# Softmax factors moved into the queries, and no scaling of the row maxima

## The chip, the cores and the metric

The kernel runs on one core of one Trainium2 chip. The metric is device time in microseconds (us), from one launch; three runs of the kernel before took 1216.63 to 1222.46 us, median 1217.19. Engines are named as in the profile: PE (TensorE), PEld (its weight loads), DVE (VectorE), ACT (ScalarE), POOL (GpSimd), SP (SyncE, which issues most DMAs).

## The reference

Two blocks on 256 tokens of 1024 features, all in fp32. The first block has two layers, each a softmax attention and a squared-ReLU MLP; the second has a gated feed-forward layer, a mixer (a state-space product beside a latent attention) and another gated layer. Three attentions appear, and each scales its logits before the softmax:

```python
# layer 0 (16 heads of 64): scale = 1/sqrt(64)
s_own = einsum('bhcd,bhkd->bhck', qc, k_own) * scale - slopes * dist_own       # causal
# layer 1: scale = 1/sqrt(64), c = running sum of log forget gates
sc = einsum('bhqd,bhkd->bhqk', qb, k) * scale + cq[..., None] - c[:, :, None, :]  # causal
# latent attention (8 heads of 64 + 32): scale = 1/sqrt(96)
q = (rmsnorm(cq, q_norm_w) @ w_uq)
s = (einsum(q_nope, k_nope) + einsum(q_rope, k_rope)) * scale                     # causal
p = softmax(s); out = p @ v
```

## The kernel before, in words

Every product with a weight is made in three passes of float32r (hi hi, hi lo, lo hi), by token (lines 212 to 214) or by feature (245 to 247). So each slab of weights, 128x1024 values, is loaded by SP into `raw` (line 147, five buffers), cast by ACT to `wh` and subtracted to `wl`: lines 174 and 175 without a gain, 178 and 179 with one. The subtraction of line 175 is done by DVE, or by POOL for the slabs listed in `on_pool`; the output weights of both attention layers are mostly such. At most five slabs are made ahead of PE.

The program is written out in one order for all engines, and each engine takes its instructions in that order. Big products go on, and side chains (generators) advance by a step at each `tick()`. An attention is such a chain. It works by halves of a PSUM bank of scores: six halves per group of 8 heads (four heads with 128 keys, or two with 256), two groups per layer, and six halves for the latent attention, 30 in all. One half goes through these steps:

- PE makes the scores from `qT` and `kT` (line 607; 1276 in the latent attention).
- DVE adds bias and mask from PSUM to SBUF, `pr` (622, 629 or 1283), takes the negative row maxima `m` (532), and multiplies them by the softmax factor (534). Up to here the logits are 8 (or sqrt(96)) times too large.
- ACT takes the exponentials with that factor as `scale`, and their sums `sm` (537).
- DVE takes the reciprocals (541, or 551 in the latent attention). In the first block POOL then divides (542).
- PE transposes `pr` (547), ACT copies the result to `pT` (549), and PE multiplies by the values (641; 567 in the latent attention).

`queries` (711) moves queries and keys from PSUM to SBUF and multiplies them by the tokens' norms, one [128, 512] tile at a time: 4 tiles of q and 4 of k in each of the two layers. In layer 1 `forget_bias` makes the running sums of the log forget gates times 8 (`lf8`, `ACT.mul(c, p, 8.0)`). In the mixer `latent_chain` makes 1/rms of the latents of queries (`rq`) and of keys (`rk`).

Between the attentions lie MLPs; beside their weights DVE adds up the second block's modulation (485), which POOL sums over the partitions (490). At their end line 846 adds the MLP to the residual `h`.

Of the kernel before, what the change touches and what calls it, by code (L numbers as in the profile page):

```python
# [12 lines left out]
AF = mybir.ActivationFunctionType  # L13
# [3 lines left out]
S = 256  # L17
# [11 lines left out]
def kernel(ctx: ExitStack, tc: tile.TileContext, a: dict, out: bass.AP):  # L29
# [68 lines left out]
    def finish(*some):  # L98
        """Emits what is left of these chains."""
        while any(s in sides for s in some):  # L100
            for s in some:
                if s in sides:
                    advance(s)

    def after_all(*some):
        """Waits for these chains."""
        while any(s in sides for s in some):
            yield 1

# [9 lines left out]
    def slab(w, r0, nk, c0, n, gain=None, m=None, early=0):  # L119
        """Rows r0 .. r0+128*nk and columns c0 .. c0+n of w, in parts of m rows of blocks, the first few split early,  # L120
        into tiles that are free then."""
# [12 lines left out]
    def load_ahead(most=RB):  # L134
        while at["dma"] < min(len(plan), at["prep"] + most):
# [10 lines left out]
            if at["dma"]:  # L146
                nc.sync.dma_start(raw, src)
            else:
                # the first product waits for no more than it needs
                for k in range(src.shape[1]):  # L150
                    nc.sync.dma_start(raw[:, k], src[:, k])
# [32 lines left out]
    def take(i):  # L184
        """Slab i, and more made ready behind it."""
# [19 lines left out]
    def by_t(xT, t):  # L205
        """The stationary operands of token tile t: [(hi, lo)] by k."""
        return [(x[0][:, j, tok(t)], x[1][:, j, tok(t)]) for x in xT for j in range(4)]

    def part(p, xs, ws, first, last):
        """p += x @ w, by token."""  # L210
# [5 lines left out]
    def by_token(idx, xs, ps, first=True, last=True, token_first=False, after=None, before=None):  # L216
        """ps[t] += x[t] @ slab; xs[t]: [(hi, lo)] by k."""
# [15 lines left out]
    def by_feature(idx, xT, ps, before=None):  # L233
        """ps: [128, 2, 256] each; (x @ w)^T, by blocks of 128 columns of w."""
        k = 0
        for i in idx:
            if before is not None:
                before(k)
            for wh, wl in take(i):
                xh, xl = (z[:, k % 4, :] for z in xT[k // 4])  # L240
                for n in range(2 * len(ps)):
                    c = slice(n * TP, (n + 1) * TP)
                    o = ps[n // 2][:, n % 2, :]
                    # the bank's first product clears both halves' flags, so the other half's first overwrites
# [12 lines left out]
    def split(hi, lo, src):  # L257
        """An activation, split into two exact parts."""
# [12 lines left out]
    def transposed(bl, tag):  # L271
        """Up to 4 [128, 128] blocks, transposed and split; returns [(hi, lo)] by block."""
# [13 lines left out]
    def hidden_part(q):  # L286
        """Hidden activations [128, 2, 256], split: [(hi, lo)] by block."""
# [12 lines left out]
    def mean_square(parts, n, eps=EPS):  # L300
        """mean of squares along the free axis, plus eps."""
# [18 lines left out]
    def warm(func):  # L320
        """Has ScalarE load the table of a function ahead of its use."""
# [9 lines left out]
    def log1p_of(e, shape):  # L331
        """log(1 + e) for 0 <= e <= 1, as 2 atanh(e / (2 + e))."""
# [23 lines left out]
    def columns(n, parts, queue):  # L356
        """Rows of 128 values as columns: [128, n]."""
# [15 lines left out]
    def keep_warm(n):  # L373
        """TensorE's clock is at half speed until it has been busy for some microseconds."""
# [25 lines left out]
    def plan_hidden(ups, w_down, cuts, rate, early=0, after=0):  # L400
        """Weights of the cuts of a hidden layer; each cut's last product is one step behind its first ones."""
# [64 lines left out]
    ada = {}  # L466

    def ada_begin(n):
        """The bias in one partition, nothing in the others."""
# [28 lines left out]
    def modulation(j):  # L498
        """A shift, gain or gate of a sublayer, on every partition."""
# [13 lines left out]
    # ticks between the halves of an attention, and within each: before its logits, sums, transposes and products  # L513
# [4 lines left out]
    def attention(halves_, scores, biased, values, put, ready_v=lambda: True, pace=None, give=None):  # L518
        """halves_: (t, n heads, key); scores(i) emits the scores of half i (and says which others it made);
        biased(i, pr, sc) their logits and scale; values(i) the values; put(i, o, rs) takes the products.  # L520
        With give, the probabilities are divided by their sums and given to it by twos of halves, transposed."""
# [3 lines left out]
        def half(s):  # L525
# [4 lines left out]
            scale = biased(s, pr, sc.pop(s))  # L530
            m = tt((TP, nh), "m")
            DVE.tensor_reduce(out=m, in_=pr, axis=AX.X, op=OP.max, negate=True)
            if scale != 1.0:
                DVE.tensor_scalar(m, m, scale, None, op0=OP.mult)
            sm, rs = tt((TP, nh), "sm"), tt((TP, nh), "rs")
            for i in range(nh):
                ACT.activation(out=pr[:, i, :], in_=pr[:, i, :], func=AF.Exp, bias=m[:, i:i + 1], scale=scale,
# [52 lines left out]
    # ================= the first block =================  # L590
    HALVES = [(0, 4, 0, 0), (0, 4, 0, 1), (1, 2, 0, 0), (1, 2, 0, 1), (1, 2, 4, 0), (1, 2, 4, 1)]

    def heads_attention(g, q, k, v, bias, mixT):
        """8 heads of 64 of group g; q, k: by 4 heads, [128, 2, 256]; v: by key tile."""
# [20 lines left out]
        def biased(i, pr, sc):  # L615
            t, nh = HALVES[i][:2]
            if bias is None:
                # 8 * (q k / 8 - slope * distance), causal
                d = dist if t == 1 else dist[:, TP:S]
                for j in range(nh):  # L620
                    slope = 2.0 ** (-8.0 * (8 * g + head(i, j) + 1) / H)
                    DVE.scalar_tensor_tensor(out=pr[:, j, :], in0=d, scalar=-8.0 * slope, in1=sc[:, j, :],
                                             op0=OP.mult, op1=OP.add)
                return 0.125
            # 8 * (q k / 8 + c[query] - c[key]), causal
# [5 lines left out]
            return 0.125  # L631

        def give(i, pT):
            # the values of each head of a pair on a half of the columns: the products come out transposed
# [20 lines left out]
    def attention_layer(layer, ids, xT, vs, chains, next_chain):  # L655
        """xT, vs: made by chains[t][s]; next_chain(t, s): what follows on each part of the residual."""
# [938 lines left out]
```

## Time and profile before

| | |
|---|---|
| runs of the kernel before | 1216.63, 1217.19, 1222.46 us |
| profiled execution: span | 1219.5 us (the page gives no other time of this execution) |
| PE busy | 1174.3 us, 96% |
| DVE busy | 865.2 us, 71% |
| ACT busy | 650.9 us, 53% |
| POOL busy | 304.3 us, 25% |
| mean granted clock of PE | 0.984 of full speed |

The page tells busy time of each engine, the span in 40 slices, the DMA queues, the chain of work that ended last and the costliest groups of instructions. A row of a timeline has the start and the duration in us, then engine, line, operation and tiles; a bracket at its end is the idle time of that engine just before, and what ended it. [...]

### The profile page before, as it was taken

To read this page: it belongs to the slowest core of one execution; us is meant where nothing else is said; L and a number is where in the kernel's file an instruction comes from. 1 tells how busy PE (TensorE), PEld (TensorE's weight loads), DVE (VectorE), ACT (ScalarE), POOL (GpSimd) and SP (SyncE) were. 2 spreads that over 40 slices of the span, in tenths; PEclk is the share of its full clock that TensorE was granted. 3 is DMA by queue.
4 is the path that set the end of the run, shared out by engine and by line. 5 is a ranking of instruction groups with operands and counts; after the bars stand their busy time and mean duration, and the time that the engine had idled before them with its cause. 6 is when DMAs were issued, how large, how long until landed. Compare 5 with 4: busy or idle time off the path is not lost.

```text
span 1219.5 us, 19985 instructions
## 1 busy us (share of the span) xinstructions
PE 1174.3 (96%) x7669; PEld 1059.2 (87%) x7669; DVE 865.2 (71%) x1218; ACT 650.9 (53%) x1115; POOL 304.3 (25%) x260
## 2 busy tenths in 40 slices
PE   8999999999999999999989999998998999999997
PEld 8977989988899789989878999988987787899996
DVE  6665678887677568778777877756776776766445
ACT  6565665445555665455545444545765564444443
POOL 3054202133002511211153112154136405111002
PEclk9999999999999999999989999999998999999999
DMA  8642467886553347878846888853632263777650
GB/s 277 194 127 99 157 226 236 274 275 223 184 172 123 105 130 235 288 264 299 284 143 214 292 268 312 276 176 118 220 89 88 93 226 111 270 232 228 222 189 36
DMA packets 128479, 243.04 MB, mean 199 GB/s; under 512 B 8515, under 2 KB 16612, under 8 KB 128384
## 3 DMA queue, kind: packets, MB, share of 16 engines
q1 hardware_dynamic: 126688, 239.96, 59.7%
q0 software_dynamic: 1376, 1.28, 0.5%
q8 instruction: 60, 0.98, 0.3%
q10 hardware_dynamic: 320, 0.53, 0.1%
q14 instruction: 35, 0.29, 0.1%
HBM read 240.65 MB, written 1.09 MB: 198 GB/s over the span
## 4 chain that ended last, share of the span: by engine, by line
PE 64%; DVE 16%; ACT 6%; DMA 6%; issue 5%; POOL 3%; SPq 0%; POOLq 0%; ACTq 0%; DVEq 0%
PE mm L247 8%; PE mm L246 8%; PE mm L245 8%; PE acc L212 7%; PE acc L213 7%; PE acc L214 7%; DVE wl L179 4%; DMA raw<-in_w_down_dram 3%; PE acc L245 3%; PE acc L247 3%; PE acc L246 3%; DVE wl L175 2%; ACT wh L174 2%; PE mm L213 2%; PE mm L212 2%
## 5 line engine op out<-in xcount | busy, mean ns | idle before, releaser
L174 ACT CAST wh<-raw 128x1024 fp32r<-128x1024 f32 (+1 forms) x231 | 237.7, 1041 | 221.0 <-DMA raw<-in_w_down_dram 67.2
L175 DVE TENSOR_TENSOR wl<-raw,wh 128x1024 fp32r<-128x1024 f32 (+1 forms) x193 | 257.8, 1350 | 137.2 <-ACT wh L174 134.8
L247 PE MATMUL mm<-xh,wl 128*128 128x256 f32 x1088 | 309.3, 284 | 4.4 <-DVE wl L179 4.3
L245 PE MATMUL mm<-xh,wh 128*128 128x256 f32 x1088 | 309.1, 284 | 0.1
L246 PE MATMUL mm<-xl,wh 128*128 128x256 f32 x1088 | 308.4, 283 | 0.0
L179 DVE SCALAR_TENSOR_TENSOR wl<-raw,cols,wh 128x512 fp32r<-128x512 f32 (+1 forms) x270 | 204.0, 806 | 68.0 <-ACT wh L178 64.5
L247 PEld LDWEIGHTS mm<-xh,wl 128*128 128x128 f32 x1088 | 209.3, 192 | 5.9 <-DVE wl L179 5.9
L245 PEld LDWEIGHTS mm<-xh,wh 128*128 128x128 f32 x1088 | 209.3, 192 | 1.3 <-ACT wh L178 0.6
L246 PEld LDWEIGHTS mm<-xl,wh 128*128 128x128 f32 x1088 | 209.3, 192 | 0.7
L178 ACT ACTIVATE wh<-raw,cols 128x512 fp32r<-128x512 f32 (+1 forms) x270 | 175.3, 708 | 64.5 <-PE acc L246 20.1
L212 PE MATMUL acc<-wh,mh 128*128 128x512 f32 x524 | 207.6, 396 | 0.0
L213 PE MATMUL acc<-wl,mh 128*128 128x512 f32 x524 | 205.4, 392 | 0.0
L214 PE MATMUL acc<-wh,ml 128*128 128x512 f32 x524 | 205.1, 391 | 0.0
L490 POOL PARTITION_ALL_REDUCE ada<-ada x18 | 66.4, 3690 | 352.1 <-DVE ada L485 153.4
L175 POOL TENSOR_TENSOR wl<-raw,wh 128x1024 fp32r<-128x1024 f32 (+1 forms) x38 | 91.4, 2407 | 138.9 <-ACT wh L174 132.3
L214 PEld LDWEIGHTS acc<-wh,ml 128*128 128x128 f32 x524 | 99.0, 189 | 21.1
L212 PEld LDWEIGHTS acc<-wh,mh 128*128 128x128 f32 x524 | 98.9, 189 | 20.8 <-issue 1.7
L213 PEld LDWEIGHTS acc<-wl,mh 128*128 128x128 f32 x524 | 99.1, 189 | 19.0 <-DVE wl L175 0.2
L485 DVE SCALAR_TENSOR_TENSOR ada<-raw,c_act,ada 128x512 f32<-128x512 f32 x144 | 107.7, 748 | 2.5
L245 PE MATMUL acc<-xh,wh 128*128 128x256 f32 x352 | 102.0, 290 | 0.0
L246 PE MATMUL acc<-xl,wh 128*128 128x256 f32 x352 | 99.5, 283 | 0.0
L247 PE MATMUL acc<-xh,wl 128*128 128x256 f32 x352 | 99.5, 283 | 0.0
(318 smaller groups left out, 1673.5 us busy)
## 6 DMA issues: line engine op xcount, KB each, us to landing
raw<-in_w_ada_dram SPq DMA_DIRECT2D x72, 512.0 KB, 5.4
raw<-in_w_up_dram SPq DMA_DIRECT2D x64, 512.0 KB, 4.9
raw<-in_w_down_dram SPq DMA_DIRECT2D x64, 512.0 KB, 5.7
raw<-in_ffn_w_gate_dram SPq DMA_DIRECT2D x44, 512.0 KB, 4.7
raw<-in_ffn_w_up_dram SPq DMA_DIRECT2D x44, 512.0 KB, 4.7
raw<-in_ffn_w_down_dram SPq DMA_DIRECT2D x44, 512.0 KB, 5.2
raw<-in_moba_w_qkv_dram SPq DMA_DIRECT2D x23, 512.0 KB, 5.0
raw<-in_w_in_dram SPq DMA_DIRECT2D x20, 512.0 KB, 4.1
```

What stands on the lines that cost most here:

```text
L174: ACT.copy(hi, raw)
L175: (POOL if i in on_pool else DVE).tensor_tensor(lo, raw, f(hi), op=OP.subtract)
L178: ACT.mul(hi[:, k], raw[:, k], gain[k])
L179: DVE.scalar_tensor_tensor(out=lo[:, k], in0=raw[:, k], scalar=gain[k], in1=f(hi[:, k]), op0=OP.mult, op1=OP.subtract)
L212: PE.matmul(p, lhsT=xh, rhs=wh, start=first and n == 0, stop=False)
L213: PE.matmul(p, lhsT=xh, rhs=wl, start=False, stop=False)
L214: PE.matmul(p, lhsT=xl, rhs=wh, start=False, stop=last and n == len(ws) - 1)
L245: PE.matmul(o, lhsT=wh[:, c], rhs=xh, start=k == 0 and n % 2 == 0, stop=False)
L246: PE.matmul(o, lhsT=wh[:, c], rhs=xl, start=False, stop=False)
L247: PE.matmul(o, lhsT=wl[:, c], rhs=xh, start=False, stop=k == 7 and n % 2 == 1)
L485: DVE.scalar_tensor_tensor(out=acc, in0=raw[:, i, :], scalar=c_act[:, k:k + 1], in1=acc, op0=OP.mult, op1=OP.add)
L490: POOL.partition_all_reduce(acc, acc, TP, ReduceOp.add)
```

## The change

The factor 1/8 of the first block's attentions moves into the queries, at the instruction that takes them out of PSUM; keys go through the same instruction with a factor of 1. The bias of layer 0 and the sums of layer 1 lose their factor 8. The factor 1/sqrt(96) moves into the latent queries' norm (96 under the root). The row maxima are then right as they are: line 534 goes, and the exponentials have no `scale`. Comments of the kernel also change; they are left out below.

```diff
             pr = sb("pr", (TP, nh, (t + 1) * TP))
-            scale = biased(s, pr, sc.pop(s))
+            biased(s, pr, sc.pop(s))
             m = tt((TP, nh), "m")
             DVE.tensor_reduce(out=m, in_=pr, axis=AX.X, op=OP.max, negate=True)
-            if scale != 1.0:
-                DVE.tensor_scalar(m, m, scale, None, op0=OP.mult)
             sm, rs = tt((TP, nh), "sm"), tt((TP, nh), "rs")
             for i in range(nh):
-                ACT.activation(out=pr[:, i, :], in_=pr[:, i, :], func=AF.Exp, bias=m[:, i:i + 1], scale=scale,
+                ACT.activation(out=pr[:, i, :], in_=pr[:, i, :], func=AF.Exp, bias=m[:, i:i + 1],
                                accum_out=sm[:, i:i + 1])
...
                     slope = 2.0 ** (-8.0 * (8 * g + head(i, j) + 1) / H)
-                    DVE.scalar_tensor_tensor(out=pr[:, j, :], in0=d, scalar=-8.0 * slope, in1=sc[:, j, :],
+                    DVE.scalar_tensor_tensor(out=pr[:, j, :], in0=d, scalar=-slope, in1=sc[:, j, :],
                                              op0=OP.mult, op1=OP.add)
-                return 0.125
+                return
...
                                          op0=OP.add, op1=OP.add)
-            return 0.125
...
                 o = sb("q", (TP, 2, S), name=n + "T")
-                DVE.tensor_tensor(o, p, rrow[0].unsqueeze(1).to_broadcast([TP, 2, S]), op=OP.mult)
+                DVE.scalar_tensor_tensor(out=o, in0=p, scalar=0.125 if n == "q" else 1.0,
+                                         in1=rrow[0].unsqueeze(1).to_broadcast([TP, 2, S]), op0=OP.mult, op1=OP.mult)
                 got.append(o)
...
         DVE.scalar_tensor_tensor(out=lf, in0=y, scalar=0.0, in1=l1, op0=OP.min, op1=OP.subtract)
-        lf8 = sb("ra", (TP, 2, TP), name="lf8")
-        POOL.memset(lf8, 0.0)
+        lfn = sb("ra", (TP, 2, TP), name="lfn")
+        POOL.memset(lfn, 0.0)
         for i in range(0, TP, 32):
-            DVE.tensor_scalar(lf8[:, :, i:i + H], lf, -8.0, None, op0=OP.mult)
+            DVE.tensor_scalar(lfn[:, :, i:i + H], lf, -1.0, None, op0=OP.mult)
         yield 4
...
             PE.matmul(p[:, t, :], lhsT=upper, rhs=lf[:, t, :], start=True, stop=t == 0)
-            PE.matmul(pT[:, tok(t)], lhsT=lf8[:, t, :], rhs=upper, start=True, stop=t == 0)
+            PE.matmul(pT[:, tok(t)], lhsT=lfn[:, t, :], rhs=upper, start=True, stop=t == 0)
             if t == 1:
                 PE.matmul(p[:, t, :], lhsT=ones, rhs=lf[:, 0, :], start=False, stop=True)
-                PE.matmul(pT[:, tok(t)], lhsT=lf8[:, 0, :], rhs=ones, start=False, stop=True)
+                PE.matmul(pT[:, tok(t)], lhsT=lfn[:, 0, :], rhs=ones, start=False, stop=True)
         bias["query"] = c = const.tile([TP, 2, H], F32, name="c")
-        ACT.mul(c, p, 8.0)
+        ACT.copy(c, p)
         bias["key"] = k = const.tile([TP, S], F32R, name="ck")
...
             yield 4
-            r[t] = rsqrt(total(ss, 1, EPS))
+            v = tt((TP, 1), "v")
+            POOL.tensor_scalar(v, ss[:, 0:1], EPS, 96.0 if r is rq else 1.0, op0=OP.add, op1=OP.mult)
+            r[t] = rsqrt(v)
             dst[t] += transposed(blocks(x, n), "m")
...
             DVE.tensor_tensor(pr, sc, mk, op=OP.add)
-            return 1.0 / math.sqrt(96.0)
```

DVE's order in the first attention, from the fifth half of group 0 to the end of the first half of group 1 (`pr` logits, `m` maxima, `rs` reciprocals, `ml` low part of the mixed values). Before:

```order
38 L622 SCALAR_TENSOR_TENSOR pr<-dist,mm 128x256 x2
39 L532 TENSOR_REDUCE m<-pr 128x2
40 L534 TENSOR_SCALAR m<-m 128x2
41 L541 RECIPROCAL rs<-sm 128x2
42 L622 SCALAR_TENSOR_TENSOR pr<-dist,mm 128x256 x2
43 L532 TENSOR_REDUCE m<-pr 128x2
44 L534 TENSOR_SCALAR m<-m 128x2
45 L622 SCALAR_TENSOR_TENSOR pr<-dist,mm 128x128 x4
46 L532 TENSOR_REDUCE m<-pr 128x4
47 L534 TENSOR_SCALAR m<-m 128x4
48 L260 TENSOR_TENSOR ml<-mm,mh 128x512
49 L541 RECIPROCAL rs<-sm 128x2
```

Now:

```order
34 L620 SCALAR_TENSOR_TENSOR pr<-dist,mm 128x256 x2
35 L532 TENSOR_REDUCE m<-pr 128x2
36 L539 RECIPROCAL rs<-sm 128x2
37 L620 SCALAR_TENSOR_TENSOR pr<-dist,mm 128x256 x2
38 L532 TENSOR_REDUCE m<-pr 128x2
39 L620 SCALAR_TENSOR_TENSOR pr<-dist,mm 128x128 x4
40 L532 TENSOR_REDUCE m<-pr 128x4
41 L260 TENSOR_TENSOR ml<-mm,mh 128x512
42 L539 RECIPROCAL rs<-sm 128x2
```

The maxima go to ACT from the reduction itself; nothing else has changed its place, and line numbers behind 532 are smaller by two or three.

DVE's order in the latent attention, from the second half to the third (`ym` the attention's result, `xf` the convolution). Before:

```order
563 L1283 TENSOR_TENSOR pr<-mm,mask 128x512
564 L532 TENSOR_REDUCE m<-pr 128x4
565 L534 TENSOR_SCALAR m<-m 128x4
566 L1295 TENSOR_TENSOR ym<-mm,rs 128x512
567 L551 RECIPROCAL rs<-sm 128x4
568 L1283 TENSOR_TENSOR pr<-mm,mask 128x512
569 L532 TENSOR_REDUCE m<-pr 128x2
570 L534 TENSOR_SCALAR m<-m 128x2
571 L1196 SCALAR_TENSOR_TENSOR xf<-acc,cols_123,xf 128x255
```

Now:

```order
538 L1284 TENSOR_TENSOR pr<-mm,mask 128x512
539 L532 TENSOR_REDUCE m<-pr 128x4
540 L1295 TENSOR_TENSOR ym<-mm,rs 128x512
541 L549 RECIPROCAL rs<-sm 128x4
542 L1284 TENSOR_TENSOR pr<-mm,mask 128x512
543 L532 TENSOR_REDUCE m<-pr 128x2
544 L1197 SCALAR_TENSOR_TENSOR xf<-acc,cols_123,xf 128x255
```

Here too only the multiplication of `m` has gone; the convolution and the next half's mask move up. DVE has 30 rows of this order fewer in all; on PE, ACT, POOL and SP each instruction stands where it stood.

## Rows read from the trace of the kernel before

**Rows 1.** Page, part 1: busy us (share of the span), instructions.

```profile
PE 1174.3 (96%) x7669; PEld 1059.2 (87%) x7669; DVE 865.2 (71%) x1218; ACT 650.9 (53%) x1115; POOL 304.3 (25%) x260
```

**Rows 2.** PE's waits, whole run: engine line <- releaser: us, times, longest us.

```profile
PE mm L641 <- ACT pT L549: 5.3, 5, 2.0
PE mm L547 <- POOL pr L542: 4.8, 2, 2.5
PE mm L247 <- DVE wl L179: 4.3, 6, 1.7
PE mm L547 <- ACT pr L537: 1.8, 2, 1.1
```

**Rows 3.** Busy VectorE of line 534 alone, by stretch: window, length, busy (count).

```profile
45.00:130.00 85.00, 9.34 (x12) 0.98 0.37 120
370.00:480.00 110.00, 7.95 (x11) 0.97 0.44 143
870.00:960.00 90.00, 4.05 (x6) 0.96 0.34 105
```

**Rows 4.** Timeline, 79.5 to 82.6 us: start, us, engine, line, form [idle before].

```profile
79.59 0.69 DVE L532 TENSOR_REDUCE m<-pr 128x2 f32<-128x512 f32 x1
79.71 2.40 POOL L175 TENSOR_TENSOR wl<-raw,wh 128x1024 fp32r<-128x1024 f32 x1 [2.23 <-ACT wh L174]
...
80.31 1.82 DVE L534 TENSOR_SCALAR m<-m 128x2 f32<-128x2 f32 x1
...
82.23 0.51 ACT L537 ACTIVATE pr<-pr,m 128x256 f32<-128x256 f32 x1 [2.11 <-DVE m L534]
```

**Rows 5.** Timeline, 84.3 to 95 us, all engines.

```profile
86.18 1.04 ACT L174 CAST wh<-raw 128x1024 fp32r<-128x1024 f32 x1
...
87.30 2.35 POOL L175 TENSOR_TENSOR wl<-raw,wh 128x1024 fp32r<-128x1024 f32 x1 [0.55 <-ACT wh L174]
...
90.70 0.66 PE L547 MATMUL mm<-ident,pr 128*128 128x128 f32 x4 [2.52 <-POOL pr L542]
...
91.29 3.61 PE L641 MATMUL mm<-pT,vtok 128*64 128x128 f32 x32
```

**Rows 6.** Timeline of PE, 82 to 83.5 us.

```profile
82.17 1.09 PE L641 MATMUL mm<-pT,vtok 128*64 128x128 f32 x16
```

**Rows 7.** Stretches: busy us of PE, PEld, DVE, ACT, POOL; clock; DMA; GB/s.

```profile
85.00:95.00 10.00, 7.48 (x54) 5.90 (x53) 3.72 (x10) 6.39 (x21) 6.09 (x4) 0.83 0.34 110
400.00:410.00 10.00, 7.71 (x56) 6.07 (x55) 3.76 (x11) 6.48 (x21) 5.76 (x4) 0.83 0.32 106
```

**Rows 8.** Timeline, 105.5 to 117 us, all engines.

```profile
106.50 1.09 PE L641 MATMUL mm<-pT,vtok 128*64 128x128 f32 x14 [0.57 <-ACT pT L549]
106.65 1.78 DVE L534 TENSOR_SCALAR m<-m 128x2 f32<-128x2 f32 x1
...
112.31 1.26 DVE L534 TENSOR_SCALAR m<-m 128x2 f32<-128x2 f32 x1
...
115.89 0.56 ACT L549 COPY pT<-mm 128x512 f32<-128x512 f32 x1
...
116.51 0.76 PE L641 MATMUL mm<-pT,vtok 128*64 128x128 f32 x9 [1.97 <-ACT pT L549]
```

**Rows 9.** Timeline of PE, 405 to 407 us.

```profile
405.41 1.11 PE L547 MATMUL mm<-ident,pr 128*128 128x128 f32 x4 [2.29 <-POOL pr L542]
```

**Rows 10.** Timeline of PE, 431 to 438 us.

```profile
431.23 1.09 PE L641 MATMUL mm<-pT,vtok 128*64 128x128 f32 x14 [1.95 <-ACT pT L549]
```

**Rows 11.** Groups by form: line, engine, form, count | busy us, mean ns.

```profile
L846 DVE SCALAR_TENSOR_TENSOR h<-acc,r,h 128x512 f32<-128x512 f32 x8 | 5.9, 743 | 3.6 <-PE acc L214 3.6
...
L711 DVE TENSOR_TENSOR qT<-acc,rrow 128x512 f32<-128x512 f32 x8 | 5.2, 685 | 0.2
```

**Rows 12.** Page, part 5: GpSimd's all-reduce.

```profile
L490 POOL PARTITION_ALL_REDUCE ada<-ada x18 | 66.4, 3690 | 352.1 <-DVE ada L485 153.4
```

**Rows 13.** Line 179, all its instructions: duration ns min/median/max.

```profile
L179 DVE SCALAR_TENSOR_TENSOR wl<-raw,cols,wh x270: 602/746/2733, 6.6 to 1005.8; 128x512 fp32r<-128x512 f32 x128, 128x384 fp32r<-128x384 f32 x7
```

## The prediction

> **What bounds the kernel.** I read the page's first part, then PE's own waits over the whole run, then the waits of the line that is removed, then the timeline around it. PE is busy for 1174.3 of the profiled 1219.5 us [rows 1], so the kernel can gain only what stands in PE's gaps, or PE running at the full clock where it does not now. Softmax accounts for three rows of those gaps [rows 2]: 5.3 us in which the products with the values (L641) wait for a transposed probability copied by ScalarE, 4.8 us in which a transpose (L547) waits for GpSimd's division, and 1.8 us in which a transpose waits for an exponential itself. Together 11.9 us. The diff touches every chain that ends in one of them.
>
> The reader is next to look at L534, the tiny multiplication of the maxima (128x2 or 128x4 values). Twelve of them take 9.34 us in the first attention, eleven take 7.95 in the second (the twelfth lies just ahead of that window), six take 4.05 in the third [rows 3]: 21.3 us for 29 instructions, 0.74 us each, for work that has next to no elements. The timeline shows why [rows 4]. The maximum (L532) runs 79.59 to 80.28, while a GpSimd subtraction runs 79.71 to 82.11, and is not held up. L534 starts at 80.31 and ends at 82.13, 0.02 us behind the GpSimd operation. The exponential, for which ScalarE had been idle 2.11 us, starts at 82.23. So L534 does not take 1.82 us: it stands still until GpSimd's operation has ended, VectorE and ScalarE with it.
>
> [...]
>
> **The change part by part.**
>
> *The scaling of the maxima (30 instructions).* VectorE's list loses exactly these; the other engines' lists keep their order. VectorE loses 21.3 us of occupied time, but it is not the bound. What counts is how far each PE gap shrinks.
>
> (a) The transposes that wait for GpSimd, two gaps, 4.8 us. The first ends at 90.70 after 2.52 us [rows 5], the second at 405.41 after 2.29 [rows 9]. The first goes back over GpSimd's subtraction at 87.30, which could not begin before ScalarE's cast ended (86.18 + 1.04 = 87.22). Without L534 the exponential of [rows 4] could start at 80.31 + 0.10 instead of 82.23, 1.82 sooner, and I take ScalarE's operations between there and the cast to follow at most that much sooner. They may be held back by products that have yet to read a buffer, and GpSimd by the operation ahead. So each gap shrinks by 0 to 1.82; I take 1.4, nearer to the upper end because ScalarE's start moves by the full 1.82. Two gaps: 2.8 us.
>
> (b) The clock behind these two gaps. [...] In the first one 32 products of L641 take 3.61 us [rows 5]; 16 of them take 1.09 at the upper level [rows 6], so 32 would take 2.18, and 1.43 us are lost. If the shrunk gap (2.52 - 1.4 = 1.1 us) does not bring the clock down, that comes back. 0 to 1.43 each; I take 1.4, as PE is what the work behind it waits for: 2.8 us.
>
> (c) The products that wait for copied probabilities, 5.3 us in five gaps. In the first attention 0.57 us end at 106.50 and 1.97 at 116.51 [rows 8], in the second one of 1.95 ends at 431.23 [rows 10]. Take the second of [rows 8]: its last piece is ScalarE's copy at 115.89, which is queued behind the exponential, and that behind L534 of 112.31 (1.26 us) and, one half earlier, L534 of 106.65 (1.78 us). Both go, 3.04 us together, more than the 1.97 of the gap. What is late next is PE itself: the transposes that feed the copy are its own earlier work. The bounds are 0 and 5.3; I take 4.2, which leaves the small gaps in which a copy follows directly on transposes.
>
> (d) The latent attention. Six L534 take 4.05 us [rows 3]; PE waits 1.8 us in two gaps for an exponential [rows 2]. 0 to 1.8; I take the middle, 0.9, because GpSimd is at work there nearly all the time and VectorE's convolution shares the queue.
>
> *The factor in the queries.* Sixteen evacuations of q and k become SCALAR_TENSOR_TENSOR. The nearest row of that form with a PSUM input, L846, has 743 ns, the TENSOR_TENSOR of L711 685 [rows 11]: 16 x 58 ns = 0.93 us of VectorE. It could cost up to that, or nothing, or gain nothing. I take 0: no row of PE's waits names a query or a key, since the scores come after a further slab of products; without that cover it is 0.9 us.
>
> *The rest.* The latent query norm has the same GpSimd operation with a second factor, the forget bias a copy instead of a multiplication by 8: the same instructions in the same places. The nearest price of a second factor is the 58 ns just named; for two such instructions in the norm and one in the bias that is under 0.2 us either way; I take 0. No DMA, and no step past a queue, is moved.
>
> Sum against the profiled execution: 2.8 + 2.8 + 4.2 + 0.9 = 10.7 us less than its 1219.5 us span. The runs lie from 1216.63 to 1222.46 with a median of 1217.19, which is 2.3 us under that span, so the profiled execution was one of the longer ones; the gaps do not depend on that, and I take the difference off the median: 1217.19 - 10.7 = 1206.5 us.
>
> **The rivals.** A measurement of this kernel tells about 0.5% from no change, 6.1 us: the bounds are 1211.1 and 1223.3.
>
> Rival 1, the wait changes hands. The next VectorE operation that needs what GpSimd holds stands still instead, or GpSimd behind ScalarE's casts stays as late as before, so that the gaps of (a) and the clock remain. For it: in [rows 5] the division waits behind a subtraction of GpSimd's own, 2.35 us. Against it: what follows L534 on VectorE is a maximum's input or a reciprocal, and the reduction of [rows 4] runs through. Then only (c) is left, half to all of it: 2.7 to 4.2 us, some 1213.5 us.
>
> [...]
>
> Rival 2, everything opens. All three waits vanish and the clock stays up, behind the gap at 431.23 too: 11.9 + 3 x 1.43 = 16.2 us, 1201.0 us. Against it: a transpose must still follow its GpSimd division, and that its cast.
>
> Rival 3, given back. PE comes some 5 us sooner to each hidden layer and waits there for VectorE's low parts (4.3 us of PE's waits now, [rows 2]). Half of the gain goes: 1212 us. Against it: at most five slabs of weights are made ahead of PE, so that VectorE follows PE's pace.
>
> Rival 4, slower. The shifted work puts GpSimd's all-reduces (18, 3.69 us each [rows 12]) against the weight subtractions L179 just before their first use. These take 746 ns in the middle and 2733 at most [rows 13], so one collision costs 2 us, and 1.4 more where the clock falls. It has to give back 10.7 and add 6.1 us, five new collisions of the eighteen with all of it on PE's path.
>
> That the change does not do what it says is hardly a rival: the row is gone from VectorE's list.
>
> **How the numbers follow.** Forecast (1203 to 1210) 0.57; rival 1 0.15, rival 2 0.13, rival 3 0.12, rival 4 0.03. The range reaches from rival 2's end to a little past rival 1's: 1200.5 to 1214. Faster by over 0.5% are the forecast, rival 2 and half of rival 3: 0.76; same 0.21; slower 0.03.
>
> **What would show it.** PE's waits for GpSimd's division and for copied probabilities fall from 10.1 us to about 3; the exponentials no longer wait behind VectorE while GpSimd is at work; the clock is 1.00 behind the first attention's middle. I am wrong in (a) and (b) if the gap near 90 us stays above 2 us, in (c) if the one near 116 stays, and in the whole if VectorE's weight subtractions grow by what L534 loses.

## The result, and the profile after

The changed kernel takes 1201.93 us (median of six runs, 1195.19 to 1203.44). The kernel before, run beside it, takes 1217.62 (six runs, 1216.51 to 1222.46). The ratio is 0.9848, with a 95% interval of 0.9831 to 0.9866. On the 1217.19 us shown above that is 1198.7 us: 18.5 us gained where 10.7 were forecast, and 1.8 us below the low end of the range. The ratio is not that of the two medians, which is 0.9871: by the medians themselves the gain is 15.7 us, and 1201.93 lies inside the range. By either figure the change is faster and the gain larger than forecast; what it rests on was named rightly, its size was not.

The profiled execution after took 1202.77 us, with a span of 1201.1. Against the span of before, 18.4 us are gone, and they fall into two parts. Page, part 1 of the changed kernel (engine, busy us, share of the span, instructions):

```profile
PE 1163.7 (97%) x7669; PEld 1051.3 (88%) x7669; DVE 847.7 (71%) x1188; ACT 652.0 (54%) x1115; POOL 301.3 (25%) x260
```

PE has the same 7669 instructions as in [rows 1], so its idle time fell from 1219.5 - 1174.3 = 45.2 us to 1201.1 - 1163.7 = 37.4: 7.8 us less. Its busy time fell by 10.6 us for the same work. That second part is the reader's first lesson here: a count of PE's gaps cannot show it. VectorE is busy 17.5 us less (the scaling operations are gone, its weight subtractions take 3.3 us more), and that is no part of the sum. The pair of traces serves to place the gain; their 18.4 us agree with the 18.5 above by chance, since single runs of the changed kernel differ by up to 8 us.

**The gaps.** PE's waits in the changed kernel (engine line <- releaser: us in total, times, longest us):

```profile
PE mm L265 <- DVE hn L980: 9.9, 4, 4.1
PE mm L247 <- DVE wl L179: 5.1, 6, 1.4
PE mm L265 <- DMA h<-in_x_dram: 2.2, 1, 2.2
...
PE mm L1360 <- ACT th L1201: 1.2, 1, 1.2
...
PE mm L545 <- POOL pr L540: 1.0, 2, 0.6
...
PE mm L545 <- ACT pr L535: 0.9, 1, 0.9
PE mm L638 <- ACT pT L547: 0.7, 2, 0.4
...
PE mm L1339 <- ACT xs L1220: 0.3, 1, 0.3
```

The last of them was, in the same view of the kernel before:

```profile
PE mm L1339 <- ACT xs L1219: 1.8, 1, 1.8
```

The lines have moved up by two or three: L545 is the transpose that was L547, L638 the value product that was L641; from line 1339 on, lines added in between make up for it. Against [rows 2] the wait for GpSimd's division fell from 4.8 to 1.0 us, that for copied probabilities from 5.3 to 0.7, that for an exponential from 1.8 to 0.9: 9.3 us together. The low parts (L179) took 0.8 us of it back. The weight subtractions on VectorE did not inherit the standstill (page, part 5: line, form, count | busy us, mean ns | idle before):

```profile
L175 DVE TENSOR_TENSOR wl<-raw,wh 128x1024 fp32r<-128x1024 f32 (+1 forms) x193 | 261.0, 1368 | 135.1 <-ACT wh L174 132.1
...
L179 DVE SCALAR_TENSOR_TENSOR wl<-raw,cols,wh 128x512 fp32r<-128x512 f32 (+1 forms) x270 | 204.1, 807 | 68.2 <-ACT wh L178 68.2
```

L179 took 204.0 us before, L175 257.8: of the 21.3 us that L534 held, at most 3.3 can have gone there.

Where L534 stood, the timeline of the changed kernel, 78.5 to 82 us, reads (start, us, engine, line, form, idle before):

```profile
79.56 0.69 DVE L532 TENSOR_REDUCE m<-pr 128x2 f32<-128x512 f32 x1
79.67 2.38 POOL L175 TENSOR_TENSOR wl<-raw,wh 128x1024 fp32r<-128x1024 f32 x1 [1.26 <-ACT wh L174]
...
80.36 0.51 ACT L535 ACTIVATE pr<-pr,m 128x256 f32<-128x256 f32 x1
```

The reduction and GpSimd's subtraction lie as in [rows 4], but the exponential starts at 80.36, 1.69 us before the subtraction ends at 82.05. In [rows 4] it started 0.12 us after the subtraction ended. Further on, the answer to [rows 5], from the timeline of 82 to 94 us:

```profile
86.58 2.38 POOL L175 TENSOR_TENSOR wl<-raw,wh 128x1024 fp32r<-128x1024 f32 x1 [1.19 <-ACT wh L174]
...
90.02 0.66 PE L545 MATMUL mm<-ident,pr 128*128 128x128 f32 x4 [0.62 <-POOL pr L540]
90.60 2.00 PE L638 MATMUL mm<-pT,vtok 128*64 128x128 f32 x32
```

The subtraction begins 0.72 us sooner, the transposes 0.68 (90.02 against 90.70), and PE waits 0.62 us instead of 2.52. By the clock of the two traces PE arrives 1.2 us later here; that is no effect of the gap, for this execution was 1.7 us behind from its start (below). An execution without that lag, that of experiment 5, whose kernel is the changed one in this stage, has the same wait:

```profile
87.71 0.66 PE L547 MATMUL mm<-ident,pr 128*128 128x128 f32 x4 [0.62 <-POOL pr L542]
```

Its transposes start 2.99 us sooner than before. So against PE's own work GpSimd's division comes 1.9 us sooner. The products behind the gap show the other part: the 32 that took 3.61 us now take 2.00.

**The clock.** Busy us of PE, PEld, DVE, ACT and POOL, then the granted clock, DMA share and GB/s, in stretches that begin and end with the same instruction in both kernels: first attention, second attention, latent attention. Before:

```profile
49.11:117.53 68.42, 63.36 (x443) 52.87 (x441) 43.22 (x92) 39.08 (x102) 28.35 (x19) 0.98 0.36 116
370.10:446.02 75.92, 71.09 (x474) 58.37 (x472) 47.82 (x96) 43.56 (x109) 26.85 (x19) 0.96 0.34 109
884.33:950.10 65.77, 59.45 (x400) 52.39 (x398) 48.36 (x83) 39.58 (x90) 36.69 (x24) 0.95 0.29 89
```

Of the changed kernel, the same three, and a stretch in the MLP between the first two:

```profile
50.86:111.81 60.95, 60.33 (x442) 50.71 (x441) 34.51 (x80) 40.01 (x102) 28.32 (x19) 1.00 0.42 130
362.87:430.82 67.95, 67.13 (x474) 55.47 (x472) 39.95 (x85) 44.11 (x108) 26.81 (x19) 1.00 0.38 120
870.27:931.71 61.44, 56.38 (x400) 50.01 (x398) 44.30 (x77) 39.13 (x90) 36.71 (x24) 1.00 0.32 96
270.00:280.00 10.00, 7.76 (x48) 6.75 (x47) 9.02 (x11) 7.31 (x12) 3.58 (x1) 1.00 0.51 170
```

The first attention is 7.5 us shorter (4.4 in gaps, 3.0 in PE's busy time), the second 8.0 (4.0 and 4.0), the latent attention 4.3 (1.3 and 3.1). The clock has two levels here. In windows of 1 us of the kernel before it reads 1.00 from 84 to 91 us, 0.64, 0.50, 0.50 and 0.65 from 91 to 95, and 1.00 in the two behind; from 925 to 930 us it reads 0.50 throughout. A mean between the two is taken as a mix of them. At 0.50 the products of L212 to L214 start 0.43 us apart (925.84 to 927.98 us), at 1.00 0.23 us (95.17 to 95.87).

Where the lower level stood, beside the two stretches of [rows 7], the kernel before shows it in that MLP, behind the gap of [rows 10], and in the latent attention:

```profile
278.00:288.00 10.00, 7.89 (x46) 6.82 (x45) 9.28 (x12) 6.59 (x10) 3.58 (x1) 0.83 0.47 149
425.00:440.00 15.00, 12.94 (x78) 9.82 (x77) 7.30 (x14) 7.91 (x18) 4.44 (x3) 0.89 0.27 91
900.00:930.00 30.00, 25.04 (x166) 22.39 (x165) 20.34 (x38) 18.29 (x43) 20.41 (x15) 0.90 0.35 106
```

Five stretches thus lost the lower level, not two: 0.17 x 10 / 0.5 = 3.4 us at 0.50 in each of three, 0.11 x 15 / 0.5 = 3.3 in the fourth, 0.10 x 30 / 0.5 = 6 in the fifth, 19.5 us together. The profiled execution after has 3.4 us of its own at 8.5 us (0.50 from 9 to 11 us), behind the wait for the first input (2.2 us; 1.5 before). Over the whole span the mean clock rose from 0.984 to 0.991: 39.0 against 21.6 us at the lower level, 17.4 less. By the 0.43 and 0.23 us just named that is 17.4 x (1 - 0.23 / 0.43), an estimated 8 us of PE's time, and most of the 10.6 us that PE was busy less. Part of the rest lies beside the gaps: the sixteen value products around the gap of [rows 10] take 0.43 us (two) and 1.09 us (fourteen) before, and 1.23 us in one piece after, so the closed gap of 1.95 us gave 0.3 us more than its length.

These figures are of one pair of executions, and the clock differs between executions of one kernel. The 0.984 is below that of 33 other executions of the kernel before (0.985 to 0.992, in the middle 0.988), and the 0.991 is the lowest of the changed kernel's six (0.991 to 0.996, in the middle 0.993). By the middle values the time at the lower level fell by some 12 us (29 to 17), not 17.

Matching instructions show where the lead arises. At its first attention the changed kernel was 1.7 us behind (50.86 against 49.11). The transposes that start at 117.53 us before start at 111.81 after, 5.7 us sooner: 7.5 us come from the first attention. The MLP behind it gives 1.5, the second attention 8.0; what lies between it and the latent attention takes 1.1 back; the latent attention gives 4.3, with the new wait behind it (L1360) counted.

### The profile page after: what moved, and what is told of

The parts are those of the page before. It is cut to its first block, busy times and chain, and to the rows that moved or that the text cites. A ratio compares the mean times of both kernels' runs of the same rounds, so it can differ in the third digit from the quotient of the medians.

```text
span 1201.1 us, 19954 instructions
## 1 busy us (share of the span) xinstructions
PE 1163.7 (97%) x7669; PEld 1051.3 (88%) x7669; DVE 847.7 (71%) x1188; ACT 652.0 (54%) x1115; POOL 301.3 (25%) x260
## 3 DMA queue, kind: packets, MB, share of 16 engines
HBM read 240.65 MB, written 1.09 MB: 201 GB/s over the span
## 4 chain that ended last, share of the span: by engine, by line
PE 65%; DVE 16%; DMA 7%; ACT 6%; issue 4%; POOL 2%; SPq 0%; POOLq 0%; DVEq 0%; ACTq 0%
PE mm L247 8%; PE mm L246 8%; PE mm L245 8%; PE acc L212 8%; PE acc L213 7%; PE acc L214 7%; DVE wl L179 4%; DMA raw<-in_w_down_dram 4%; PE acc L245 3%; PE acc L247 3%; PE acc L246 3%; DVE wl L175 3%; ACT wh L174 2%; DVE ada L485 2%; PE mm L212 2%
## 5 line engine op out<-in xcount | busy, mean ns | idle before, releaser
L175 DVE TENSOR_TENSOR wl<-raw,wh 128x1024 fp32r<-128x1024 f32 (+1 forms) x193 | 261.0, 1368 | 135.1 <-ACT wh L174 132.1
L179 DVE SCALAR_TENSOR_TENSOR wl<-raw,cols,wh 128x512 fp32r<-128x512 f32 (+1 forms) x270 | 204.1, 807 | 68.2 <-ACT wh L178 68.2
L212 PE MATMUL acc<-wh,mh 128*128 128x512 f32 x524 | 207.4, 396 | 0.0
L214 PE MATMUL acc<-wh,ml 128*128 128x512 f32 x524 | 205.0, 391 | 0.0
L175 POOL TENSOR_TENSOR wl<-raw,wh 128x1024 fp32r<-128x1024 f32 (+1 forms) x38 | 91.5, 2410 | 130.8 <-ACT wh L174 125.6
L214 PEld LDWEIGHTS acc<-wh,ml 128*128 128x128 f32 x524 | 98.8, 189 | 21.0
L212 PEld LDWEIGHTS acc<-wh,mh 128*128 128x128 f32 x524 | 98.9, 189 | 20.6 <-issue 1.6
```

Of the source, the lines that this page charges most:

```text
L175: (POOL if i in on_pool else DVE).tensor_tensor(lo, raw, f(hi), op=OP.subtract)
L179: DVE.scalar_tensor_tensor(out=lo[:, k], in0=raw[:, k], scalar=gain[k], in1=f(hi[:, k]), op0=OP.mult, op1=OP.subtract)
L212: PE.matmul(p, lhsT=xh, rhs=wh, start=first and n == 0, stop=False)
L214: PE.matmul(p, lhsT=xl, rhs=wh, start=False, stop=last and n == len(ws) - 1)
```

## The experiments

All stand on the changed kernel unless the text says otherwise. Ratios are to the kernel before, with 95% intervals; the changed kernel's is 0.9848 [0.9831, 0.9866].

**1. Is it the scaling at all?** The tiny multiplication put back, with a factor of 1; everything else of the change stays.

```diff
     DVE.tensor_reduce(out=m, in_=pr, axis=AX.X, op=OP.max, negate=True)
+    DVE.tensor_scalar(m, m, 1.0, None, op0=OP.mult)
```

> The changed kernel with one instruction put back: VectorE multiplies the maxima by 1.0 in place, in front of the exponentials. The factors stay in the queries. Theory A (the instruction stands still until GpSimd's operation ends, and the exponentials with it): the time goes back to the kernel before, 1217 us within 3 us, and the 30 instructions take about 21 us in all as they did. Rival B (the gain comes from the queries' and norms' part, or from chance in the clock): it stays near 1201 us.

Measured: 1218.6 us (median of ten), ratio 1.0 [0.9981, 1.0018]. The whole gain is gone. The waits are back too (view of PE's waits):

```profile
PE mm L639 <- ACT pT L548: 5.6, 6, 1.9
PE mm L546 <- POOL pr L541: 4.8, 2, 2.5
```

The instruction itself, all of its line (count: duration ns min/median/max, first and last start, forms; below it, who waited for it, us and times):

```profile
L533 DVE TENSOR_SCALAR m<-m x30: 169/172/1893, 53.2 to 927.3; 128x2 f32<-128x2 f32 x20, 128x4 f32<-128x4 f32 x10
...
  ACT pr L536: 69.6, 28
```

A median of 172 ns beside a maximum of 1893 for the same shapes: the operation is nearly free by itself, and some of the thirty stand still. In this trace the sixteen that meet no GpSimd operation take 0.17 us each; the fourteen that start while one runs take 0.22 to 1.89 us and end with it.

The clock is a second finding of this run. Around the places of the stretches near 282 and 431 us of before:

```profile
278.00:288.00 10.00, 7.55 (x55) 6.90 (x54) 9.56 (x12) 6.35 (x11) 3.58 (x1) 1.00 0.53 158
425.00:440.00 15.00, 12.67 (x82) 9.67 (x81) 7.81 (x14) 8.41 (x20) 4.34 (x3) 1.00 0.26 81
```

Two of the five stretches are not there, though the multiplication stands, and though PE waits 1.94 us near 430 as it did before. The span is 1219.4 us all the same (1219.5 before). So that these two went with the change is not shown. Nor did their absence bring this execution anything: PE is idle for 1219.4 - 1172.4 = 47.0 us of it, 1.8 more than before.

From the time it follows that the rest of the change (the factor at q and k, in the norm, the exponential without its scale) is worth nothing within 0.2%, as the prediction took it.

**2. Is it the standstill, or a link more in the chain?** A chain of the same length, its second link a reduction over one element.

```diff
-    DVE.tensor_reduce(out=m, in_=pr, axis=AX.X, op=OP.max, negate=True)
+    m0 = tt((TP, nh), "m0")
+    DVE.tensor_reduce(out=m0, in_=pr, axis=AX.X, op=OP.max, negate=True)
+    DVE.tensor_reduce(out=m, in_=m0.unsqueeze(2), axis=AX.X, op=OP.max)
```

> The changed kernel with another tiny instruction in the same place of the chain: a second reduction, over one element, copies the maxima to another tile. The chain is as long as in the kernel before (30 instructions of about 0.17 us), but a reduction was not held up by GpSimd. Theory A: within 2 us of the changed kernel, 1199 to 1204 us, and no one of the 30 takes over 0.3 us. Rival C (the chain was simply one instruction too long): most of the gain is lost, 1212 us or more.

Measured: 1201.77 us, ratio 0.9855 [0.984, 0.987], the changed kernel's. Its line, in the same view:

```profile
L534 DVE TENSOR_REDUCE m<-m x30: 154/155/158, 54.0 to 908.8; 128x2 f32<-128x2 f32 x20, 128x4 f32<-128x4 f32 x10
...
  ACT pr L537: 54.1, 26
```

Thirty instructions in the same place, on the same values, and none takes over 158 ns, though sixteen of them run beside a GpSimd operation. The extra link costs nothing that can be told (0.9855 against 0.9848); what cost the gain in experiment 1 was a form that stood still.

**3. Whose standstill counts, VectorE's or the exponentials'?** The same multiplication, on a tile of ones that nothing else reads.

```diff
+    side = const.tile([TP, 4], F32)
+    POOL.memset(side, 1.0)
...
     DVE.tensor_reduce(out=m, in_=pr, axis=AX.X, op=OP.max, negate=True)
+    DVE.tensor_scalar(side[:, 0:nh], side[:, 0:nh], 1.0, None, op0=OP.mult)
```

> The changed kernel with 30 multiplications of a tile of ones behind the maxima, which nothing waits for; the exponentials take the maxima from the reduction. VectorE stands still as before, but ScalarE doesn't wait for it. Theory A: both count, since the standstill also delays VectorE's next logits; I expect between, 1204 to 1212 us, with about 20 us spent in the 30 instructions. If VectorE's own standstill counts for nothing: 1199 to 1203. If it is all: 1215 to 1218.

Measured: 1201.27 us, ratio 0.9852 [0.9826, 0.9878].

```profile
L535 DVE TENSOR_SCALAR side<-side x30: 157/328/2010, 52.5 to 905.6; 128x2 f32<-128x2 f32 x20, 128x4 f32<-128x4 f32 x10
...
  ACT pr L538: 11.0, 5
```

The exponentials' other wait, for the reduction itself (what ended ScalarE's idle time before L538):

```profile
  DVE m L534: 40.0, 23
```

VectorE is held as long as ever (the thirty instructions take 22.7 us, against 21.5 in the first experiment), and the kernel loses nothing that can be told. ScalarE waits 51.0 us ahead of the exponentials in all, near the changed kernel's 48.0 and not the 69.6 of experiment 1. I had expected both to count; what shows in the time is the exponentials' wait.

**4. How much is the clock by itself?** The kernel before, its waits left as they are, with products that no one reads in PE's gaps: ten transposes of the identity ahead of the transposes behind the gaps of [rows 5] and [rows 9], eight ahead of value products.

```diff
+    if give is not None and s == 5 and pace is PACE[0]:
+        for _ in range(10):
+            PE.transpose(p[:, 0, :], ident, ident)
...
+    if g == 1 and i == 2:
+        for _ in range(8):
+            PE.transpose(o[:, 0, :], ident, ident)
```

> The kernel before, with 10 transposes of the identity ahead of the waiting transposes of the sixth half of group 0, and 8 ahead of the products of halves 2 and 3 of group 1, in both layers: PE is busy for 0.8 to 1.1 us of each of the four long gaps, and each is that much shorter. Theory A with the clock as its larger part: the stretches at the lower clock behind the gaps near 91, 405 and 432 us go, 1.4 to 1.7 us each, so 1213 us with the gaps' ends unmoved (4 to 5 us less than before). If the clock falls for another reason than the gaps: no change, 1217, or up to 1 us more.

Measured: 1215.02 us, ratio 0.9977 [0.9962, 0.9992]: a gain of 2.8 us (1.0 to 4.6). PE's timeline, 85.8 to 92.5 us, shows a filled gap:

```profile
89.09 1.31 PE L547 MATMUL mm<-ident 128*128 128x128 f32 x10
91.47 0.66 PE L550 MATMUL mm<-ident,pr 128*128 128x128 f32 x4 [1.07 <-POOL pr L542]
```

and its stretches, those of [rows 7] first:

```profile
85.00:95.00 10.00, 8.63 (x70) 6.44 (x69) 3.88 (x11) 7.60 (x26) 6.76 (x4) 1.00 0.40 137
400.00:410.00 10.00, 8.80 (x72) 6.93 (x72) 5.43 (x14) 6.10 (x16) 4.59 (x4) 1.00 0.36 106
425.00:440.00 15.00, 13.52 (x91) 10.57 (x90) 7.55 (x13) 9.27 (x21) 2.92 (x3) 1.00 0.33 106
```

The granted clock is 1.00 in all three, and the transposes still start late (91.47). So the clock is a gain of its own, apart from the wait. It is smaller than the 4 to 5 us that I expected from three stretches. In the profiled execution the two attentions, between the instructions used above, are 1.3 us (49.87 to 117.02) and 2.2 us (368.88 to 442.63) shorter, 3.4 in all; a part goes where PE, faster behind the gap, reaches the next wait sooner, but that was not measured by itself. Span and mean clock of this execution:

```profile
core 0: 1213.9 us, clock 0.992
```

The changed kernel has 1201.1 us at 0.991. At nearly the same mean clock, then, 12.8 of the 18.4 us between the two profiled executions are still missing while the waits stand: the clock without the waits gives the smaller part.

**5. How much is the latent attention?** The multiplication of experiment 1, in the third attention alone (six of the thirty).

```diff
+    if give is None:
+        DVE.tensor_scalar(m, m, 1.0, None, op0=OP.mult)
```

> The changed kernel with the multiplication by 1.0 put back in the latent attention alone (6 of 30). The trace of the changed kernel is 4 to 5 us further ahead behind the latent attention than ahead of it, where the prediction counted 0.9. Theory A with the clock: about 4 us of the gain go, 1205 us, and the 6.8 us at the lower clock near 910 us come back. If the prediction's own size was right: 1202 to 1203 us.

Measured: 1204.25 us, ratio 0.9881 [0.9855, 0.9906]: 0.33%, some 4 us, of the gain is gone, though the intervals overlap. Its waits:

```profile
PE mm L547 <- ACT pr L537: 1.8, 2, 1.1
PE mm L1341 <- ACT xs L1222: 1.8, 1, 1.8
```

Both are back at the figures of before (1.8 and 1.8; 0.9 and 0.3 after). That is 2.4 us of waits. The lower clock near 910 us, which I expected back, did not come in the profiled execution (stretch of 884 to 916 us):

```profile
884.00:916.00 32.00, 26.84 (x188) 23.37 (x187) 22.15 (x40) 20.59 (x48) 22.40 (x16) 1.00 0.33 100
```

That makes the run a test of the clock too: the clock of after with the waits of before. The latent attention between the same instructions as above:

```profile
867.99:932.97 64.98, 57.18 (x399) 50.02 (x398) 48.29 (x83) 39.22 (x90) 36.67 (x24) 1.00 0.29 90
```

Before it took 65.77 us, in the changed kernel 61.44. Of the 4.3 us, then, 3.5 go with the multiplication at an unchanged clock, and 0.8 are left to the clock.

**6. Does the same lever reach further?** The changed kernel's largest wait left is L265 for the modulated inputs, 9.9 us in four gaps, and behind three of them the clock falls (0.80, 0.86 and 0.79 in stretches of 17, 12 and 8 us from 613, 808 and 998 us on). Products that no one reads again, ahead of the first transposes of three sublayers' inputs: `fill` is 28 in the chain of two norms and 14 in that of one, which two sublayers use.

```diff
-    def transposed_into(hi, lo, blocks):
+    def transposed_into(hi, lo, blocks, fill=0):
         p = mm_ps((TP, len(blocks), TP))
+        for _ in range(fill):
+            PE.transpose(p[:, 0, :], ident, ident)
...
-    def modulated(xT, t, src, ys, r, shift):
+    def modulated(xT, t, src, ys, r, shift, fill):
...
-        into_xT(xT, t, 0, blocks(ys[0]))
+        into_xT(xT, t, 0, blocks(ys[0]), fill if t == 0 else 0)
```

> The changed kernel with transposes of the identity ahead of the first transposes of three sublayers' inputs (28, 14 and 14 of them), where PE idles 4.1, 2.5 and 2.7 us for the norm and where the clock falls for 6.8, 3.4 and 3.4 us behind. The gaps' ends do not move. Theory: the clock alone is worth up to half of these 13.6 us, I expect 5 us, so some 1196 us. If the lower clock is not due to the idle gap, or nothing behind it waits for PE: 1201 us as without, or 1 us more.

Measured: 1194.6 us (1192.52 to 1195.47), ratio 0.9809 [0.9794, 0.9824]. It beats both kernels, the changed one by some 0.4%, with intervals that do not overlap. Span and mean clock of the core, and PE's wait that was 9.9 us:

```profile
core 0: 1190.8 us, clock 0.998
```

```profile
PE mm L267 <- DVE hn L982: 3.6, 4, 1.1
```

The wait shrinks because the filling counts as work; the inputs come no sooner for it. What is gained is the clock, 0.998 over the whole span. The two profiled executions are 10.3 us apart, but between matching instructions the three filled stages give only 1.9, 1.7 and 1.6 us; the rest lies where the edit does nothing, a difference between executions. The 5 us of the three agree with the 0.4%.

**7 and 8. More of the same.** Twenty dummy products at the very start in place of ten (`keep_warm(20)`), and, in another kernel, one weight subtraction less on GpSimd (the entry `(F1[0][0][0], (3,))` taken off its list), both on top of experiment 6.

> The kernel of x6 with 20 instead of 10 transposes of the identity at the very start, where some executions show a gap of 1 to 2 us for the first input and some a stretch of 3.4 us at the lower clock behind it. Expected: 0 to 2 us less than x6 in the median, and less spread. If the first input is then waited for by as much: the same.

> The kernel of x6 with one weight subtraction near 611 us moved from GpSimd to VectorE. In the changed kernel a VectorE multiplication with two SBUF inputs takes 2.70 us there under this GpSimd operation (2.85 us) and 0.69 us elsewhere. If such an operation stands still as the maxima did: about 1 us less than x6, because VectorE then has 1.2 us of the subtraction itself. If it does not matter: the same; if VectorE's 1.2 us weigh more: 1 us more.

Measured: 1197.2 us, ratio 0.9831 [0.9812, 0.9851], and 1192.79 us, ratio 0.98 [0.9785, 0.9816]. Neither can be told from experiment 6. The second shows the standstill in another form. VectorE's multiplication of two SBUF operands, L1026, at that place in experiment 6 (timeline):

```profile
606.27 2.70 DVE L1026 TENSOR_TENSOR h<-u,mod 128x512 f32<-128x512 f32 x1
```

and in experiment 8, where GpSimd's subtraction beside it is gone:

```profile
608.41 0.69 DVE L1026 TENSOR_TENSOR h<-u,mod 128x512 f32<-128x512 f32 x1
```

Its time fell by 2.01 us, and the kernel's did not follow beyond what can be told.

**9. The other side of the standstill.** The multiplication stays as in experiment 1, and GpSimd's work goes: the thirteen subtractions of the two attentions' output weights run on VectorE.

```diff
-    for x, picks in ((A0["o", 0, 1], (0, 1)), (A0["o", 1, 1], (0, 1)), (A1["o", 0, 1], (0, 1)),
-                     (A1["o", 1, 1], (0, 1)), (F1[0][0][0], (3,)), ...
-                     (A0["o", 0, 0], (0, 1)), (A0["o", 1, 0], (0,)), (A1["o", 0, 0], (1,)), (A1["o", 1, 0], (1,)),
+    for x, picks in (
+                     (F1[0][0][0], (3,)), ...
```

> The kernel of x1 (multiplication by 1.0 back on all maxima), with the 13 weight subtractions of the two attention layers' output weights on VectorE instead of GpSimd. GpSimd's operations that overlap the maxima are then gone, but for its own divisions. Theory A: the 24 multiplications of the first two attentions take 0.17 us each, with few exceptions, some 5 us in all instead of 17, though nothing about them has changed; the time, with VectorE's 13 x 1.2 us more beside it, between 1203 and 1213 us. If the instruction is slow by itself: still 15 us or more in these two stages, and 1217 us or more.

Measured: 1231.19 us, ratio 1.0114 [1.0095, 1.0132]. Busy VectorE of the multiplication alone, in the three attentions (window, length, busy and count):

```profile
45.00:130.00 85.00, 2.53 (x12) 0.92 0.35 109
375.00:490.00 115.00, 2.09 (x11) 0.93 0.41 129
880.00:980.00 100.00, 4.06 (x6) 0.97 0.35 110
```

Against [rows 3] the first two fell from 9.34 to 2.53 and from 7.95 to 2.09; the third, whose GpSimd work was left alone, stayed at 4.06. So GpSimd's operation is what the multiplication stands still for. The time went the other way, and my expectation of it missed. PE's waits in this kernel:

```profile
PE mm L639 <- ACT pT L548: 7.2, 5, 2.7
PE mm L606 <- DVE ml L260: 6.3, 2, 3.2
```

VectorE now has the subtractions in its own queue, ahead of the maxima and of the low parts (L260) that the scores need, and the clock falls to 0.92 and 0.93 in these stages. Here it was dearer to carry that work on VectorE (1231.19 us) than to stand still for GpSimd now and then (1218.6 in experiment 1).

## Why the prediction was right in its mechanism and wrong in its size

- **What bounds the kernel, and what L534 does:** right. Experiments 1, 2 and 9 show it from three sides: with the multiplication the gain is gone, with a link that does not stand still it stays, and without GpSimd's work the standstill goes. No reduction was held: the thirty of L532 in the kernel before take 0.685 to 0.690 us, 24 of them beside a GpSimd operation, and the second link of experiment 2 takes 158 ns at most. What the two engines share no run shows, only which operations ended with GpSimd's.
- **(a), transposes that wait for GpSimd:** 2.8 us were forecast, 3.8 measured (4.8 to 1.0): 1.9 in each gap, over the step's own bound of 1.82. The step followed the one standstill at 80.31; ahead of it on ScalarE's path stands another, at 76.56, of 0.94 us, which it did not count. That this makes the difference was not tested.
- **(b), the clock, is the step that failed most.** The term counted the two stretches of [rows 7], 2.8 us, and took PE's busy time as unchanged elsewhere. In the two attentions alone PE was busy 7.0 us less (3.0 and 4.0). No row of the prediction gives the level at which its 16 products of [rows 6] ran; their window, 82.17 to 83.26 us, has a clock of 1.00, that of 92 to 94 us, among the 32 products, 0.50. The price of a stretch was about right (1.61 us by the 32 products that took 3.61 us and now take 2.00); the count was not: the prediction had the third, behind 431.23 us, in rival 2 alone, though the gap ahead of it, 1.95 us [rows 10], was one of those that term (c) closed. The term also left out the products beside a closed gap, which get shorter as well. The stretches near 282 and 924 us it did not list at all. That the three further stretches went because of the change is not shown: experiment 1 lacks two of them and experiment 5 the last, with the multiplication in place. Nor do PE's 10.6 us stand for the clock alone: experiment 4, with nearly the mean clock of the changed kernel, gained 2.8 us.
- **(c), products that wait for copied probabilities:** 4.2 forecast, 4.6 measured.
- **(d), the latent attention, failed beside it:** 0.9 forecast, bound 1.8. The stage became 4.3 us shorter, 3.5 of them by the multiplication at an unchanged clock (experiment 5). The wait for an exponential fell by just 0.9, but a second wait fell with it (the products behind ScalarE's copy of xs, 1.8 to 0.3), which stood outside the softmax's rows.
- **The terms of cost, all taken as 0:** right within 0.2% by experiment 1.
- **Given back:** 0.8 us at the low parts, 1.2 in a new wait for ScalarE (L1360), 0.7 at the first input. Rival 3 gave half of the gain; nothing of that size came.
- **Of the rivals,** number 1 (the wait changes hands) is refuted by the waits after, and so is the form of it in which VectorE's weight subtractions inherit the wait: another operation on two SBUF operands, L1026, does stand still (2.70 against 0.69 us, experiments 6 and 8), but L179 and L175 together took 3.3 us more. Number 2 (everything opens, 1201.0) came nearest, with a chance of 0.13: 0.9 us from the median, 2.3 from the figure by the ratio.

All waits together, 2.8 + 4.2 + 0.9 = 7.9 us forecast, came out at 7.8 net of what was given back. That agreement is luck: the gaps of the softmax closed by 9.3 us, and no term had what was given back. By stages the miss of 18.4 - 10.7 = 7.7 us between the two traces is 15.4 - 9.8 = 5.6 in the first two attentions (1.4 in gaps, 4.2 in PE's busy time), 4.3 - 0.9 = 3.4 in the latent one, and 1.5 in the MLP, less 1.7 lost at the start and 1.1 behind the second attention. By the medians of the runs the miss is smaller, 15.7 - 10.7 = 5.0 us.

Three things stay open: why filling three gaps gave 2.8 us and not the 4 to 5 of the stretches that it cleared; which of the three further stretches the change removes, and which only differ between executions; and how far the stretch of lower clock at the very start, which differs between executions, spreads the changed kernel's runs (1195.19 to 1203.44).

## What to carry to other kernels

Read a group of tiny VectorE operations by minimum, median and maximum, not by its mean: 0.17 us in the middle and 1.89 at most for the same shape can mean that some of them stand still for another engine (look at what runs beside the long ones), and if one lies between a reduction and the exponentials that PE waits for, fold its factor into an earlier operation. When gaps of PE are to close, list every stretch at a lower granted clock in all stages that may shift, and price each by its length at the lower level, 0.50 here, as an estimate: PE's busy time fell by 10.6 us here and its gaps by 7.8, but the clock alone, with the waits left, was worth 2.8. Compare stages between matching instructions, and look at the clock of several executions before a stretch is put down to a change. Where a gap must stay, products that no one reads can hold the clock (0.998 over the span of experiment 6), which was worth a further 0.4% here.

## What the runs showed of the hardware that was not expected

- Thirty tiny VectorE instructions took 22.7 us, where 0.16 us each would make 4.7, at no cost that can be told (1201.27 us against 1201.93), where no one waits for their result (experiment 3).
- A multiplication of 128x2 values takes 0.17 us without a GpSimd operation beside it and up to 2.01 with one (experiments 1 and 3), and a multiplication of two SBUF operands of 128x512 takes 0.69 or 2.70, without and with GpSimd's weight subtraction beside it (experiments 8 and 6), while a reduction to 128x2 keeps its 0.155 us (experiment 2).
- The drop of the clock was not bound to a gap alone: with PE's waits in the latent attention back at 1.8 us each, the profiled execution of experiment 5 kept 1.00 where the kernel before had 0.90, and behind a gap of 1.94 us near 430 us that of experiment 1 kept 1.00 where the kernel before, behind one of 1.95, had 0.89.
